# Third down pass of a SwiGLU block: unit 8 as seven half-size products in three of four column groups, gated sums added to the residual in DRAM

## The chip, the cores and the metric

The kernel runs on one core of a Trainium2 chip. The metric is device time in microseconds of one execution of the whole program. All matrix work is in float32, each operand cut into a high and a low part, so that one product of the reference is three matmuls on the chip (high by high, high by low, low by high).

## The reference

One layer of a bidirectional encoder: adaLN modulation, two attention mixers with gates, an output projection, and a SwiGLU channel mixer, over 512 tokens of width 2048. What matters here is its end:

```python
h2 = rms_norm(x, norm2_w[l]) * (1.0 + sc2) + sh2
ff = (jax.nn.silu(h2 @ w_ffn_gate[l]) * (h2 @ w_ffn_up[l])) @ w_ffn_down[l]
x = x + g2 * ff
return rms_norm(x, final_w)
```

`w_ffn_down` has 5632 rows and 2048 columns. `g2` is one row of 2048 numbers, the same for all tokens.

## The kernel before

**Units and column groups.** The 5632 hidden features are eleven units of 512 (0 to 10). The gated hidden values of a unit are written to DRAM (`ff_d`) by the gate and up stage. The down projection goes over them in four passes: units 0 and 1, units 2 to 5, units 6 to 9, and unit 10. Each of the first three passes goes over four column groups `cc` of 512 output columns each. A pass keeps its sum of one group (`acc`, 512 tokens by 512 columns, 1 MB) in the accumulators of PSUM, adds it to what the passes before left, and passes 1 and 2 store it to `acc_d[cc]` in DRAM. The third pass loads it again (line 1585), adds its own products, multiplies by `g2` and adds the residual `x2_d`.

**Plain units and seven-product units.** `down_group` (line 1414) does one pass over one group. A unit named in `ss` is done in the Strassen-Winograd way: the 512 by 512 hidden block and the 512 by 512 weight block are cut into quarters, and seven products of sums of quarters replace eight products of quarters. Each product is 12 matmuls of 256 columns (two of each direction, times three for the high and low parts), so such a unit is 84 matmuls, and a plain one (`plain`, line 1433) is 96. For a plain unit the weights are loaded in two transfers of 512 KB and split into high and low (`wsplit`, lines 168 and 170: ACT copies the high part, DVE subtracts for the low part). For a seven-product unit `wforms` (line 686 on) loads the same two transfers, makes four sums of quarters on DVE (lines 696 to 699) and splits four pieces, one of 512 elements a partition and three of 1024. The hidden side of such a unit is made once for all groups by `sforms` (line 1384): two loads of 512 KB, four sums (lines 1393 to 1396), four splits, into a slot that holds the result. It is a generator with two steps; the list `bg` holds those under way, and `pump` advances it by one step after every piece of work.

**Slots and areas.** There are three slots for seven-product forms. In the second pass they hold units 2, 3 and 4; units 6 and 7 take over slots 0 and 1 in its last group, and in the third pass slot 2 is free: its room is used by `xr` (a residual group and two `g2` factors) and by `fl` (the split hidden values of unit 10). Two areas hold the split hidden values of plain units (5, 8, 9).

**Order within the third pass.** Group 0 does the plain units 8 and 9 first (`lead`) and then 6 and 7; groups 1 to 3 do 6, 7 and then the plain units 8 and 9 (`tail`). While the tail runs on TensorE, DVE adds the seven products of the finished units to `acc` (lines 1471 to 1480), and after the tail four more sums (line 1485). `late(cc)` gives a function that `down_group` calls after each unit; it starts what belongs to the stage behind. In particular, after unit 7 of the next group `gated_sum` runs for the group before: two multiplications of `acc` by the factor (line 1576) and two additions of the residual (line 1577), each 128 partitions by 1024 elements; then the sum is stored to `x2p_d[cc]` (line 1579) and the next residual group and factor are loaded (lines 1569, 1570). In group 3 the stage behind is prepared: the `g2` row for all columns (`rows`, line 439), the three stored sums are loaded again (line 1557), and the weights of unit 10 are multiplied by `g2` (line 1528) and split. The last stage (line 1612 on) then does unit 10 for all columns, adds to `x2`, normalises and writes out.

**What sets the order.** Weights are loaded on SP's queue, the hidden values, `acc`, the residual and the factors on POOL's queue, each in the order of its instructions, and an instruction that waits holds up those behind it. A planner orders each engine's instructions by priority and its own costs; `high_priority` moves work ahead, and `behind` (an alias of `keep_in_program_order`) and `issue_after` tie it down. Five buffers hold loaded weights (`raw`, also used for loaded hidden values) and five hold split ones (`whl`); a seven-product unit needs two and four of them, a plain one two and two.

Of the kernel before, what the change touches and what calls it, by code (L numbers as in the profile page):

```python
# [20 lines left out]
P = 128  # L21
# [91 lines left out]
def encoder_block(ctx: ExitStack, tc, xp, xT, c, ada1_w, ada2_w, b_ada, norm1_w, w_in, q_norm_w, k_norm_w, bias,  # L113
# [1404 lines left out]
    xr = p_e.tile([P, 3072 + 64], F32, tag="s23072", name="xr")  # L1518
    xo = [xr[:, :2048].rearrange("p (i n) -> p i n", i=NT)]
    fl = p_e.tile([P, 4096 + 64], F32R, tag="s24096", name="fl")  # L1520
    wl = {}
    x2p_d = [dram.tile([P, NT, 512], F32, name=f"x2pd{cc}") for cc in range(3)]
# [9 lines left out]
    def late(cc):  # L1532
        def behind(u):
            if cc == 0 and u == 8:
                while bg:
                    pump()
            if cc == 1 and u > 7:
                a = u - 8
                xl_pairs.append(ff_pair(10, a, [fl[:, a * 2048 + e * 1024:a * 2048 + (e + 1) * 1024] for e in range(2)],
                                        pin=tc.keep_in_program_order))  # L1540
# [6 lines left out]
            if cc == 3 and u == 7:  # L1547
                x2.append(p_s.tile([P, NT, 512], F32, tag="s13072", name="xd"))
                gf = p_s.tile([P, 2, D], F32, tag="s14096", name="gf")
                wide2.extend((gf[:, 0], gf[:, 1]))  # L1550
                rows(wide2[0], g2_d)
            if cc == 3 and u == 9:
# [3 lines left out]
                for c in range(3):  # L1556
                    nc.gpsimd.dma_start(x2[c], x2p_d[c])
# [7 lines left out]
    def factor(cc):  # L1565
        return xr[:, 2048 + cc % 2 * 512:2560 + cc % 2 * 512]

    def residual_of(cc):
        nc.gpsimd.dma_start(xo[0], x2_d[:, cc * 512:(cc + 1) * 512].rearrange("(i p) d -> p i d", p=P))
        nc.gpsimd.dma_start(factor(cc), g2_d[cc].partition_broadcast(P).rearrange("p o d -> p (o d)"))  # L1570

    def gated_sum(cc, acc):
        to = xo[0] if cc < 3 else x2[3]
        for t in range(2):
            ts = slice(2 * t, 2 * t + 2)
            behind(V.tensor_mul(acc[:, ts], acc[:, ts], factor(cc).unsqueeze(1).to_broadcast([P, 2, 512])))
            behind(V.tensor_add(to[:, ts], xo[0][:, ts], acc[:, ts]))
        if cc < 3:
            nc.gpsimd.dma_start(x2p_d[cc], xo[0])
            residual_of(cc + 1)  # L1580

    residual_of(0)
    for cc in range(4):
        acc = acc_tile()
        nc.gpsimd.dma_start(acc, acc_d[cc])
        down_group(cc, (6, 7), cl, acc, late(cc), () if cc else (8, 9), late=cc > 1,
# [6 lines left out]
    for cc in range(2, 4):  # L1593
        wt = p_s.tile([P, 4096 + 64], F32R, tag=f"a{3 - cc}", name=f"w{cc}")
# [80 lines left out]
```

## Time and profile before

| what | value |
|---|---|
| median of three runs | 2465.59 us (2464.08 to 2469.82) |
| the profiled execution | 2474.1 us, span of its instructions 2472.3 us |
| TensorE busy (PE) | 2435.4 us, 99% of the span |
| DVE busy | 2007.5 us, 81% |
| ACT busy | 1069.9 us, 43% |
| granted TensorE clock, mean | 0.997 of full |
| DMA, mean over the span | 187 GB/s |

The profiled execution is 8.5 us longer than the median of the runs. The span runs from the first to the last instruction of the program; the remaining 1.8 us lie around it. The chain of waits is followed back from the last instruction; its shares tell which engine held the end, averaged over the whole program, not what holds it in the third pass. That is read from stretches of the trace. The passes were placed in it by the names of the operands of the matmuls (`s` for seven-product units, `a` for plain ones, `fl` for unit 10): the second pass begins with the first products at 2100.7 us, the third at 2258.1 us, and the last stage at 2418.9 us.

### The profile page before, as it was taken

What the parts mean: (1) busy time and instruction counts of PE and PEld (TensorE: products, weight loads), DVE (VectorE), ACT (ScalarE), POOL (GpSimd) and SP (SyncE); (2) the same over time, 40 slices, a digit from 0 to 9 for tenths busy, and PEclk for the clock granted to TensorE, in tenths of its full rate; (3) what the DMA queues carried; (4) which work ended last, traced back from release to release, by engine and by line L of the source; (5) the groups of instructions that cost most, each with busy time, mean ns of one, the idle gap of its engine ahead of it and who ended that gap; (6) DMA issues with size and microseconds to landing.
All of it is one profiled execution on the core that took longest, in us unless ns stands there. A gap on an engine that the chain in (4) does not pass through costs nothing.

```text
span 2472.3 us, 42367 instructions
## 1 busy us (share of the span) xinstructions
PE 2435.4 (99%) x17327; PEld 2280.1 (92%) x17327; DVE 2007.5 (81%) x2704; ACT 1069.9 (43%) x1466; POOL 150.9 (6%) x255
## 2 busy tenths in 40 slices
PE   7999999999999999999999999999999999999998
PEld 6888888999888888888999999999999998999997
DVE  7995778999677678667899989889989885687877
ACT  5223455544344523237744444444444454433333
POOL 0100000000011111111000000000000010000010
PEclk9999999999999999999999999999999999999999
DMA  9874322455766687867444444445454466546563
GB/s 357 285 253 144 104 89 80 142 185 181 252 211 231 204 302 248 296 215 228 137 154 155 145 162 147 135 147 163 129 171 147 128 196 214 188 155 233 189 250 121
DMA packets 213730, 461.77 MB, mean 187 GB/s; under 512 B 15152, under 2 KB 59552, under 8 KB 204832
## 3 DMA queue, kind: packets, MB, share of 16 engines
q1 hardware_dynamic: 174160, 309.76, 38.4%
q0 software_dynamic: 29872, 132.73, 15.8%
q10 hardware_dynamic: 9504, 16.58, 1.9%
q8 instruction: 136, 2.23, 0.4%
q14 instruction: 58, 0.48, 0.1%
HBM read 412.84 MB, written 46.17 MB: 186 GB/s over the span
## 4 chain that ended last, share of the span: by engine, by line
PE 72%; DVE 14%; issue 6%; DMA 4%; ACT 1%; POOL 0%; DVEq 0%; POOLq 0%; ACTq 0%
PE mm L190 15%; PE mm L189 15%; PE mm L188 15%; PE S L188 6%; PE S L189 6%; PE S L190 6%; DVE whl L170 4%; PE Y L188 3%; PE Y L189 2%; PE Y L190 2%; DVE raw L524 2%; DMA raw<-in_w_down 2%; DMA raw<-in_w_up 1%; PE T L886 1%; DVE g_acc L631 1%
## 5 line engine op out<-in xcount | busy, mean ns | idle before, releaser
L168 ACT ACTIVATE whl<-raw 128x1024 fp32r<-128x1024 f32 (+1 forms) x483 | 453.9, 943 | 671.1 <-PE mm L190 288.4
L170 DVE TENSOR_TENSOR whl<-raw,whl 128x1024 fp32r<-128x1024 f32 (+1 forms) x483 | 517.9, 1087 | 126.3 <-ACT whl L168 125.9
L168 ACT ACTIVATE whl<-ta 128x1024 fp32r<-128x1024 f32 x124 | 131.4, 1059 | 181.8 <-PE mm L190 107.6
L168 ACT ACTIVATE whl<-tb 128x1024 fp32r<-128x1024 f32 x124 | 131.4, 1060 | 174.5 <-PE S L190 109.8
L170 DVE TENSOR_TENSOR whl<-ta,whl 128x1024 fp32r<-128x1024 f32 x124 | 151.2, 1220 | 40.7 <-ACT whl L168 40.1
L388 DVE SCALAR_TENSOR_TENSOR acc<-mw,cact,acc 128x1024 f32<-128x1024 f32 x124 | 158.8, 1281 | 18.3 <-DMA mw<-in_ada_w 17.9
L170 DVE TENSOR_TENSOR whl<-tb,whl 128x1024 fp32r<-128x1024 f32 x124 | 150.9, 1217 | 4.6 <-ACT whl L168 4.5
L366 POOL DMA_DIRECT2D mw<-in_ada_w x113 | 60.3, 534 | 1361.5 <-DVE acc L388 946.5
L697 DVE TENSOR_TENSOR ta<-raw,ta 128x512 f32<-128x512 f32 x124 | 85.2, 687 | 69.3 <-DMA raw<-in_w_down 29.7
L696 DVE TENSOR_TENSOR ta<-raw 128x512 f32<-128x512 f32 x124 | 85.3, 688 | 36.7 <-DMA raw<-in_w_down 34.3
L188 PE MATMUL mm<-x56h,whl 128*128 128x256 f32 x336 | 92.5, 275 | 0.4 <-DVE c L784 0.4
L189 PE MATMUL mm<-x56l,whl 128*128 128x256 f32 x336 | 92.4, 275 | 0.0
L190 PE MATMUL mm<-x56h,whl 128*128 128x256 f32 x336 | 92.4, 275 | 0.0
L189 PE MATMUL mm<-whl,s 128*128 128x256 f32 x320 | 88.2, 276 | 1.0 <-DVE whl L170 0.8
L188 PE MATMUL mm<-x3h,whl 128*128 128x256 f32 x320 | 88.1, 275 | 0.0
L188 PE MATMUL mm<-whl,s 128*128 128x256 f32 x320 | 88.1, 275 | 0.0
L189 PE MATMUL mm<-x3l,whl 128*128 128x256 f32 x320 | 88.0, 275 | 0.0
L190 PE MATMUL mm<-x3h,whl 128*128 128x256 f32 x320 | 88.0, 275 | 0.0
L188 PE MATMUL S<-x56h,whl 128*128 128x256 f32 x320 | 88.0, 275 | 0.0
L189 PE MATMUL S<-x56l,whl 128*128 128x256 f32 x320 | 88.0, 275 | 0.0
L190 PE MATMUL S<-x56h,whl 128*128 128x256 f32 x320 | 88.0, 275 | 0.0
L190 PE MATMUL mm<-whl,s 128*128 128x256 f32 x320 | 88.0, 275 | 0.0
(1879 smaller groups left out, 8910.9 us busy)
## 6 DMA issues: line engine op xcount, KB each, us to landing
raw<-in_w_in SPq DMA_DIRECT2D x133, 512.0 KB, 4.6
mw<-in_ada_w POOLq DMA_DIRECT2D x113, 512.0 KB, 4.5
raw<-in_w_gate SPq DMA_DIRECT2D x92, 512.0 KB, 4.6
raw<-in_w_up SPq DMA_DIRECT2D x88, 512.0 KB, 4.6
raw<-in_w_down SPq DMA_DIRECT2D x88, 512.0 KB, 5.4
raw<-in_ada_w POOLq DMA_DIRECT2D x29, 1024.0 KB, 6.6
raw<-in_w_out SPq DMA_DIRECT2D x48, 512.0 KB, 5.5
ffd<-c SPq DMA_DIRECT2D x10, 1024.0 KB, 4.8
```

The lines of the kernel that those rows point to most:

```text
L168: high = pin(S.activation(hi, src, AF.Copy))
L170: latest[:] = [high, pin(eng.tensor_sub(lo, src, hi))]
L188: nc.tensor.matmul(o, lh, rh, start=start, stop=False, **kw)
L189: nc.tensor.matmul(o, lh, rl, start=False, stop=False, **kw)
L190: nc.tensor.matmul(o, ll, rh, start=False, stop=stop, **kw)
L366: mod["queue"].dma_start(w, ada2_w[n * P:(n + 1) * P, :])
L388: behind(V.scalar_tensor_tensor(acc, part, cact[:, k:k + 1], acc, op0=ALU.mult, op1=ALU.add))
L524: V.scalar_tensor_tensor(raw, raw, 1.0, call, op0=ALU.mult, op1=ALU.mult, accum_out=y)
L631: V.tensor_add(acc, acc, b)
L696: V.tensor_sub(t1, b12, b11)
L697: V.tensor_sub(t2_, b22, t1)
L886: nc.tensor.transpose(tp[:, k * P:(k + 1) * P], e[:, k * P:(k + 1) * P], ident)
```

## The change

- In groups 1 to 3 of the third pass unit 8 is done as seven products after units 6 and 7; only unit 9 stays plain there. Group 0 keeps units 8 and 9 plain, in front. The forms of unit 8 are made by `sforms` into slot 2; it is put into `bg` after unit 7 of group 0.
- `gated_sum` no longer adds on DVE for groups 0 to 2: after each multiplication a DMA on POOL's queue stores that half of `acc` (512 KB) with an addition into `x2_d`. The loads of the residual groups into `xr` and the stores to `x2p_d` go away. For group 3 DVE adds to a residual group that is loaded into `x2[3]` after unit 7 of group 3.
- The three other groups of `x2` are loaded from `x2_d` (rows of 2 KB) instead of `x2p_d` (8 KB a partition).
- `fl` moves to the area that held unit 8, and one of the last stage's weight tiles to slot 2; the factors get two small buffers of their own.

```diff
-    xr = p_e.tile([P, 3072 + 64], F32, tag="s23072", name="xr")
-    xo = [xr[:, :2048].rearrange("p (i n) -> p i n", i=NT)]
-    fl = p_e.tile([P, 4096 + 64], F32R, tag="s24096", name="fl")
-    wl = {}
-    x2p_d = [dram.tile([P, NT, 512], F32, name=f"x2pd{cc}") for cc in range(3)]
+    fl, wl = [], {}
+    x2_of = lambda cc: x2_d[:, cc * 512:(cc + 1) * 512].rearrange("(i p) d -> p i d", p=P)
...
+            if cc == 0 and u == 7:
+                bg.append(sforms(2, 8))
             if cc == 1 and u > 7:
                 a = u - 8
-                xl_pairs.append(ff_pair(10, a, [fl[:, ...
+                if a == 0:
+                    fl.append(p_s.tile([P, 4096 + 64], F32R, tag="a1", name="fl"))
+                xl_pairs.append(ff_pair(10, a, [fl[0][:, ...
...
                 rows(wide2[0], g2_d)
+                nc.gpsimd.dma_start(x2[3], x2_of(3))
...
-                    nc.gpsimd.dma_start(x2[c], x2p_d[c])
+                    nc.gpsimd.dma_start(x2[c], x2_of(c))
...
-    def factor(cc):
-        return xr[:, 2048 + cc % 2 * 512:2560 + cc % 2 * 512]
-
-    def residual_of(cc):
-        nc.gpsimd.dma_start(xo[0], x2_d[:, cc * 512:(cc + 1) * 512].rearrange("(i p) d -> p i d", p=P))
-        nc.gpsimd.dma_start(factor(cc), g2_d[cc].partition_broadcast(P).rearrange("p o d -> p (o d)"))
+    def factor_of(cc):
+        f = p_e.tile([P, 512], F32, tag="g2f", name="g2f", bufs=2)
+        nc.gpsimd.dma_start(f, g2_d[cc].partition_broadcast(P).rearrange("p o d -> p (o d)"))
+        factors.append(f)
 
     def gated_sum(cc, acc):
-        to = xo[0] if cc < 3 else x2[3]
+        f = factors.pop(0).unsqueeze(1).to_broadcast([P, 2, 512])
         for t in range(2):
             ts = slice(2 * t, 2 * t + 2)
-            behind(V.tensor_mul(acc[:, ts], acc[:, ts], factor(cc).unsqueeze(1).to_broadcast([P, 2, 512])))
-            behind(V.tensor_add(to[:, ts], xo[0][:, ts], acc[:, ts]))
+            behind(V.tensor_mul(acc[:, ts], acc[:, ts], f))
+            if cc == 3:
+                behind(V.tensor_add(x2[3][:, ts], x2[3][:, ts], acc[:, ts]))
+            else:
+                nc.gpsimd.dma_start(x2_of(cc)[:, ts], acc[:, ts], accum_op=ALU.add)
         if cc < 3:
-            nc.gpsimd.dma_start(x2p_d[cc], xo[0])
-            residual_of(cc + 1)
+            factor_of(cc + 1)
...
-        down_group(cc, (6, 7), cl, acc, late(cc), () if cc else (8, 9), late=cc > 1,
+        down_group(cc, (6, 7, 8) if cc else (6, 7), {9: cl[9]} if cc else cl, acc, late(cc), () if cc else (8, 9), late=cc > 1,
                    after_lead=cc == 1)
...
-        wt = p_s.tile([P, 4096 + 64], F32R, tag=f"a{3 - cc}", name=f"w{cc}")
+        wt = (p_e if cc == 2 else p_s).tile([P, 4096 + 64], F32R, tag="s24096" if cc == 2 else "a0", name=f"w{cc}")
```

More of the change, by code (lines that the diff above doesn't have):

```diff
@@ L1536, in behind @@
                     pump()
+            if cc == 0 and u == 7:
+                bg.append(sforms(2, 8))
             if cc == 1 and u > 7:
                 a = u - 8
-                xl_pairs.append(ff_pair(10, a, [fl[:, a * 2048 + e * 1024:a * 2048 + (e + 1) * 1024] for e in range(2)],
+                if a == 0:
+                    fl.append(p_s.tile([P, 4096 + 64], F32R, tag="a1", name="fl"))
+                xl_pairs.append(ff_pair(10, a, [fl[0][:, a * 2048 + e * 1024:a * 2048 + (e + 1) * 1024] for e in range(2)],
                                         pin=tc.keep_in_program_order))
@@ L1563, in encoder_block @@
     due = []
-    def factor(cc):
-        return xr[:, 2048 + cc % 2 * 512:2560 + cc % 2 * 512]
-    def residual_of(cc):
-        nc.gpsimd.dma_start(xo[0], x2_d[:, cc * 512:(cc + 1) * 512].rearrange("(i p) d -> p i d", p=P))
-        nc.gpsimd.dma_start(factor(cc), g2_d[cc].partition_broadcast(P).rearrange("p o d -> p (o d)"))
+    def factor_of(cc):
+        f = p_e.tile([P, 512], F32, tag="g2f", name="g2f", bufs=2)
+        nc.gpsimd.dma_start(f, g2_d[cc].partition_broadcast(P).rearrange("p o d -> p (o d)"))
+        factors.append(f)
     def gated_sum(cc, acc):
-        to = xo[0] if cc < 3 else x2[3]
+        f = factors.pop(0).unsqueeze(1).to_broadcast([P, 2, 512])
         for t in range(2):
             ts = slice(2 * t, 2 * t + 2)
-            behind(V.tensor_mul(acc[:, ts], acc[:, ts], factor(cc).unsqueeze(1).to_broadcast([P, 2, 512])))
-            behind(V.tensor_add(to[:, ts], xo[0][:, ts], acc[:, ts]))
+            behind(V.tensor_mul(acc[:, ts], acc[:, ts], f))
[3 more added lines that the diff above has]
+                nc.gpsimd.dma_start(x2_of(cc)[:, ts], acc[:, ts], accum_op=ALU.add)
         if cc < 3:
-            nc.gpsimd.dma_start(x2p_d[cc], xo[0])
-            residual_of(cc + 1)
-    residual_of(0)
+            factor_of(cc + 1)
+    factors = []
+    factor_of(0)
     for cc in range(4):
```

## The prediction

> **What bounds the kernel now.** I read the page first, then busy time by stretches, then who waited for whom in the passes concerned, then the groups of DVE instructions, then the DMA issues.
>
> ```profile
> span 2472.3 us, 42367 instructions
> PE 2435.4 (99%) x17327; PEld 2280.1 (92%) x17327; DVE 2007.5 (81%) x2704; ACT 1069.9 (43%) x1466; POOL 150.9 (6%) x255
> PE 72%; DVE 14%; issue 6%; DMA 4%; ACT 1%; POOL 0%; DVEq 0%; POOLq 0%; ACTq 0%
> ```
>
> TensorE bounds the whole program, but that is an average. The third pass is the next view: its four column groups and the last stage (span, then PE, weight loads, DVE, ACT, POOL busy, granted clock, DMA share, GB/s).
>
> ```profile
> 2258.10:2298.30 40.20, 40.20 (x362) 40.20 (x361) 30.82 (x40) 15.82 (x17) 1.61 (x3) 1.00 0.60 202
> 2298.30:2338.50 40.20, 40.20 (x362) 40.20 (x361) 35.39 (x44) 14.34 (x15) 2.91 (x5) 1.00 0.59 204
> 2338.50:2378.70 40.20, 40.20 (x362) 40.20 (x361) 30.96 (x39) 12.44 (x13) 2.39 (x4) 1.00 0.56 200
> 2378.70:2418.90 40.20, 40.20 (x362) 40.20 (x361) 28.84 (x30) 13.65 (x14) 5.03 (x9) 1.00 0.80 294
> 2418.90:2472.30 53.40, 42.23 (x206) 36.51 (x204) 42.33 (x81) 17.32 (x44) 0.00 (x0) 0.95 0.25 87
> ```
>
> In all four groups PE is busy for the whole stretch at full clock: the third pass is bound by matmuls, with nothing else in the way. So matmuls taken out there are worth their own time, as long as nothing else becomes late. DVE is at 72% to 88% of a group.
>
> The second pass already has the shape that the change gives to groups 1 to 3: three seven-product units and one plain unit. Its groups 1 to 3, and a piece of the last one:
>
> ```profile
> 2135.65:2176.07 40.42, 39.39 (x350) 39.00 (x349) 29.52 (x40) 14.14 (x15) 1.06 (x2) 1.00 0.48 160
> 2176.07:2215.33 39.26, 39.12 (x350) 38.93 (x349) 29.62 (x39) 14.08 (x15) 2.13 (x4) 1.00 0.48 161
> 2215.33:2258.10 42.77, 41.02 (x350) 40.64 (x349) 36.58 (x46) 19.09 (x21) 5.02 (x9) 0.96 0.69 229
> 2234.60:2238.00 3.40, 3.40 (x18) 0.51 0.96 327
> ```
>
> Who PE waited for in the second pass (total, times, longest):
>
> ```profile
> PE S L189 <- DVE whl L170: 1.1, 2, 0.9
> PE S L188 <- ACT whl L168: 0.9, 1, 0.9
> PE mm L189 <- DVE whl L170: 0.8, 1, 0.8
> PE T L662 <- ACT acc L1490: 0.7, 1, 0.7
> ```
>
> So in this shape PE does wait, for split weights (`whl`) of a seven-product unit.
>
> **The change, part by part.**
>
> *Matmuls.* A group of the third pass is 2 x 84 + 2 x 96 = 360 matmuls in 40.20 us, 0.1117 us each. With unit 8 as seven products it is 3 x 84 + 96 = 348, or 38.86 us. That is 1.34 us a group and 4.0 us for three: the whole of what can be gained on PE.
>
> *DVE work.* The rows of the third pass:
>
> ```profile
> L170 DVE TENSOR_TENSOR whl<-raw,whl 128x1024 fp32r<-128x1024 f32 x25 | 30.1, 1217 | 6.2 <-ACT whl L168 6.2
> L170 DVE TENSOR_TENSOR whl<-ta,whl 128x1024 fp32r<-128x1024 f32 x8 | 9.7, 1218 | 2.8 <-ACT whl L168 2.8
> L1577 DVE TENSOR_TENSOR xr<-xr,acc 128x1024 f32<-128x1024 f32 x6 | 7.3, 1222 | 0.1
> L696 DVE TENSOR_TENSOR ta<-raw 128x512 f32<-128x512 f32 x8 | 5.5, 688 | 8.4 <-DMA raw<-in_w_down 8.3
> L170 DVE TENSOR_TENSOR whl<-raw,whl 128x512 fp32r<-128x512 f32 x8 | 5.5, 683 | 0.0
> ```
>
> A seven-product unit costs DVE four sums of 0.69, one split of 0.68 and three of 1.22 us: 7.1 us. A plain unit costs two splits, 2.4 us. So each of groups 1 to 3 gains 4.7 us of DVE work. Each loses the two additions of line 1577, 2.4 us. The forms of unit 8 cost 7.1 us once (the same four sums and four splits), between unit 7 of group 0 and unit 7 of group 1. By the stretches above: groups 0 and 1 together go from 66.2 to 66.2 + 7.1 + 4.7 - 2.4 = 75.6 us of DVE in 40.20 + 38.86 = 79.06 us, 96%; group 2 to 33.3 us in 38.86 (86%); group 3 to 31.1 us (80%). On average DVE still fits. What decides is whether it fits before each unit starts, with five `whl` buffers against four that a unit needs.
>
> *What that costs in group 1.* Upper bound: group 3 of the second pass, which made the forms of two units beside three seven-product units and took 42.77 us for 348 matmuls, 3.9 us above 38.86. Of this 1.7 us is the half clock in the 3.4 us from 2234.6 (18 matmuls where 30 fit), and 2.2 us is waiting. Lower bound: 0, as 75.6 us do fit in 79. I take the middle, 2.0 us.
>
> The Trainium skill ("TensorE: Matmul & The Clock Gate", section "What's actually happening") says that the array falls to half rate after an idle window of about 3.4 us. Here it fell after waits of 2.2 us in all, so the measurement decides; the 3.4 us at half rate do agree with that window. By the page's rule the bound above would be 2.2 us, and the middle 1.1.
>
> *What it costs in groups 2 and 3.* The same shape without forms lost 40.42 - 38.86 = 1.6 us in group 1 of the second pass and 0.4 us in group 2. I take these two for the two groups, 2.0 us together; bounds 0 (DVE ahead in time) and 3.9 each (as above). The two multiplications of line 1576 come on top there, but their time is free to choose, since nothing but the store waits for them.
>
> *ACT.* Copies of high parts rise by about the same number of elements as the splits do; at 12 to 16 us of 40 it has room. Zero; were it late, DVE's splits would be late with it, which the bounds above hold.
>
> *The DMAs.* Taken out per group 0 to 2: a 1 MB load of the residual and a 1 MB store. Put in: two stores of 512 KB that add. The issues of the third pass (KB each, median us to landing), and GB/s in 40 slices of 4 us:
>
> ```profile
> GB/s 191 258 355 186 320 194 6 251 13 253 6 68 197 49 310 307 395 405 274 29 133 257 6 19 280 361 376 410 60 98 104 193 41 393 382 392 364 412 384 275
> raw<-in_w_down SPq DMA_DIRECT2D x35, 512.0 KB, 5.4
> acc<-accd POOLq DMA_DIRECT2D x3, 1024.0 KB, 7.9
> x2pd<-xr POOLq DMA_DIRECT2D x3, 1024.0 KB, 5.2
> xr<-x2d POOLq DMA_DIRECT2D x3, 1024.0 KB, 10.5
> xa<-x2pd POOLq DMA_DIRECT2D x2, 1024.0 KB, 7.4
> ```
>
> No trace shows an adding store. Bounds for 1 MB: 5.2 us (a plain store) and 5.2 + 10.5 = 15.7 us (store plus a read of those rows); I take the upper end, since the old contents have to be read. Behind it on POOL's queue stand the next factor, the load of `acc` two groups on (it now waits for the landing, as it fills the same buffer) and hidden values of unit 10. `acc` is first needed some 40 us later, so 15.7 us are covered; without that cover group cc + 2 would stand at its first sum.
>
> The Trainium skill ("Collectives: The Full Stack", section on the bandwidth ceiling) says that an add in the DMA path reads two sources and so halved a measured rate (62.28 against 32.35 GB/s). It speaks against the change; by it the store costs as 2 MB do, some 10 us, inside my bounds.
>
> *The start of the last stage.* The last seven slices above are at 275 to 412 GB/s: here DMA is full for 28 us. The waits of DVE from 2401.9 to 2424.1 and of PE from 2418.9 show it:
>
> ```profile
> DVE raw L1528 <- DMA raw<-in_w_down: 3.8, 4, 2.4
> DVE raw L1528 <- DMA gf<-g2d: 3.3, 1, 3.3
> ...
> PE S L189 <- DVE whl L170: 1.0, 1, 1.0
> PE mm L189 <- DVE w L170: 0.3, 1, 0.3
> ```
>
> PE waits 1.3 us for weights that DVE got late from DMA. The stretch opens when unit 6 of group 3 is done, which comes 2 x 1.34 = 2.7 us earlier, while PE arrives 4.0 us earlier: 1.3 us more to wait. That is the value I take. Below: the wait goes, -1.3 us. Above: 1.3 plus the read of the old 1 MB at 390 GB/s, 2.7 us, 4.0 us in all. The seven sums of group 3 also move behind unit 8, into the idle time of DVE shown here.
>
> *Sum.* -4.0 + 2.0 + 2.0 + 1.3 = +1.3 us. The durations are of one execution of 2474.1 us, 8.5 above the median; the difference is laid on the median: 2465.6 + 1.3 = 2466.9 us. The 0.2% that a measurement tells from no change is 4.9 us: 2460.7 to 2470.5. The forecast is no change, as PE gives up in waits what it saves in matmuls.
>
> **The rivals.**
>
> *The saving stays (2461.6 us, or 2460.3 with the last wait gone).* For it: in the gate and up stage DVE is as full, and PE does not wait:
>
> ```profile
> 1800.00:1900.00 100.00, 99.78 (x893) 99.60 (x892) 89.83 (x111) 43.41 (x47) 2.65 (x5) 1.00 0.49 157
> ```
>
> Against it: that stage has DMA at half and no hidden forms or sums of groups in between; the second pass, which has them, waits at 75% of DVE.
>
> *DVE becomes the bound in all three groups (slower, 2474.6 us).* Place: the splits of unit 8. Between the first form of unit 6 and the last of unit 8 DVE has 21.3 us of forms, 12 sums of a group at 0.69 (8.3 us) and the multiplications (2.4 us): 32 us against 28.1 us of PE. It decides if the lead that DVE takes from the plain unit is under 4 us, as the buffers may make it. Price: 3.9 us in each group, with the half clock: -4.0 + 11.7 + 1.3 = +9.0. Against it: two groups of the second pass lost only 0.4 and 1.6.
>
> *The adding store is slow and the last stage waits for the residual (2472 us).* The sums of group 2 are stored in group 3, and `x2` is read behind that. In the trace the first use of the third residual group is here:
>
> ```profile
> 2435.14 0.69 DVE L1608 TENSOR_TENSOR xb<-xb,ro 128x512 f32<-128x512 f32 x1
> ```
>
> The second multiplication of group 2 ends at about 2391.5. With 15.7 us for the store and 10.5 us for the load it is there by 2418, 17 us early. A store of 30 us or more with several such loads in a row would come some 5 us too late: -4.0 + 4.0 + 1.3 + 5 = +6 or so. No row speaks for that price.
>
> **How the numbers follow.** Forecast (within some 3.5 us of 2466.9): 0.47. The saving stays: 0.27. DVE bound: 0.15. Slow store: 0.11. Faster by over 0.2% needs the first rival with the last wait gone as well: 0.10. Slower by over 0.2%: nearly all of the third and fourth case: 0.22. Within: 0.68. The range goes from below the first rival's time, 2461.0, to 2473.0, short of the DVE-bound case, which leaves out about 2 in 10.
>
> **What would show it.** Right: groups 1 to 3 with 348 matmuls each; PE waits on line 170 of 1 to 3 us in group 1, under 2 in each other; a wait at the start of the last stage of 2 to 3 us. A granted clock near 0.5 for 3.4 us in group 1 would mean the upper bound there. Wrong: no PE wait on line 170 in the third pass (the first rival), waits of 2 us and half clock in all three groups (the second), DVE waiting on line 1608 for a DMA of `x2` (the third), or adding stores that land later than 16 us.

## The result and the profile after

The changed kernel takes 2496.12 us (median of 4 runs, 2493.19 to 2500.70) against 2466.61 us for the kernel before on the same chip: a ratio of 1.0121, with a 95% interval of 1.0100 to 1.0141. It is slower by some 30 us, and the forecast of no change is wrong.

The page of the kernel after: the span, the busy time of each engine, and the chain of waits by engine.

```profile
span 2495.6 us, 42337 instructions
PE 2437.1 (98%) x17291; PEld 2280.6 (91%) x17291; DVE 2018.6 (81%) x2724; ACT 1077.7 (43%) x1476; POOL 156.7 (6%) x257
PE 77%; DVE 13%; issue 3%; DMA 3%; ACT 1%; POOL 0%; DVEq 0%; POOLq 0%; ACTq 0%
```

The profile holds 36 matmuls fewer, three times 12, as the change says, and yet PE is not less busy: part of its work ran at a lower clock. The page alone does not say where the 23 us of span went. Busy time by stretches does: group 0, groups 1 to 3 and the last stage (span, then PE, weight loads, DVE, ACT, POOL, granted clock, DMA share, GB/s).

```profile
2253.60:2293.80 40.20, 40.20 (x363) 40.20 (x361) 30.81 (x40) 15.98 (x18) 2.12 (x4) 1.00 0.59 196
2293.80:2337.19 43.39, 40.62 (x350) 40.42 (x349) 36.03 (x48) 16.75 (x18) 4.74 (x6) 0.96 0.63 177
2337.19:2380.70 43.51, 41.02 (x350) 40.64 (x349) 32.99 (x43) 14.07 (x15) 3.61 (x4) 0.96 0.59 163
2380.70:2438.96 58.26, 41.92 (x350) 41.54 (x349) 34.87 (x41) 16.05 (x17) 7.75 (x10) 0.85 0.67 208
2438.96:2495.60 56.64, 43.92 (x206) 37.77 (x204) 43.56 (x82) 16.23 (x43) 0.00 (x0) 0.91 0.24 84
```

Before, the five took 40.20 four times and 53.39. So group 1 costs 3.2 us more, group 2 3.3, group 3 18.1 and the last stage 3.3: 27.8 us from the start of the third pass to the end. (The third pass starts 4.5 us earlier here than in the profile of before, which was an execution 8.5 us above its median. Of this, 4.0 us lie in the second pass, which the change leaves alone: it takes 158.6 us here and 162.6 us there, where its first product starts at 2095.5 us, not at 2100.7 as I wrote above. So I compare from the start of the third pass on.)

Group 3 is the question. Who PE waited for in groups 1 to 3, then who DVE waited for (total, times, longest):

```profile
PE Y L189 <- DVE whl L170: 15.2, 1, 15.2
PE Y L188 <- DVE acc L1485: 3.4, 2, 2.3
PE mm L189 <- DVE whl L170: 3.0, 2, 2.8
```

```profile
DVE raw L1525 <- DMA gf<-g2d: 21.9, 1, 21.9
DVE fl L170 <- ACT fl L168: 7.0, 1, 7.0
```

One wait of PE is 15.2 us long, and behind it is one wait of DVE of 21.9 us: line 1525, the product of unit 10's weights with the row of `g2` (`gf`). DVE's instructions in order of time show what stands behind it in its queue (start, duration, what, and in brackets the idle time ahead and what ended it):

```profile
2399.54 1.22 DVE L170 TENSOR_TENSOR whl<-tb,whl 128x1024 fp32r<-128x1024 f32 x1
2422.70 1.23 DVE L1525 TENSOR_TENSOR raw<-raw,gf 128x1024 f32<-128x1024 f32 x1 [21.94 <-DMA gf<-g2d]
2423.85 0.68 DVE L1471 TENSOR_TENSOR acc<-acc,p 128x512 f32<-128x512 f32 x1
2424.45 2.35 DVE L170 TENSOR_TENSOR whl<-raw,whl 128x1024 fp32r<-128x1024 f32 x2
```

The product is wanted only in the last stage, but the splits of unit 9 (2424.45), for which PE stands still in group 3, come behind it. And this is why the row is late, POOL's queue in the same time:

```profile
2392.10 0.77 POOL L1559 DMA_DIRECT2D xa<-x2d  x1 [20.47 <-PE mm L190]
2399.51 1.21 POOL L1580 DMA_DIRECT2D x2d<-acc  x1 [6.63 <-DVE whl L170]
2409.59 1.23 POOL L1580 DMA_DIRECT2D x2d<-acc  x1 [8.86 <-issue]
2416.11 0.80 POOL L1559 DMA_DIRECT2D xa<-x2d  x1 [5.30 <-issue]
2416.90 1.69 POOL L439 DMA_DIRECT2D gf<-g2d  x3
2421.92 0.54 POOL L439 DMA_DIRECT2D gf<-g2d  x1 [3.33 <-issue]
```

A load of the residual, two adding stores, another load, and only then the row. The stores and the second load each go out 0.3 us after the landing of the transfer ahead (landings at 2399.19, 2409.25 and 2415.80 us). The profile does not say so: it puts 8.86 and 5.30 us to "issue", which means to nothing that it shows, and 6.63 us to a split on DVE. In the kernel before, the first part of the row went out 3.1 us behind the store ahead of it, before that store had landed (2402.07 us):

```profile
2393.64 0.54 POOL L1579 DMA_DIRECT2D x2pd<-xr  x1 [3.93 <-DVE xr L1577]
2396.69 1.60 POOL L439 DMA_DIRECT2D gf<-g2d  x3 [2.52 <-PE S L190]
```

In groups 1 to 3 of the kernel after, the adding stores of 512 KB take this long from issue to landing (times issued, KB, median us):

```profile
x2d<-acc POOLq DMA_DIRECT2D x6, 512.0 KB, 6.3
```

### The profile page after: what moved, and what is told of

It is laid out like the page before. It is cut to its first block, busy times and chain, and to the rows that moved or that the text cites. A ratio compares the mean times of both kernels' runs of the same rounds, so it can differ in the third digit from the quotient of the medians.

```text
span 2495.6 us, 42337 instructions
## 1 busy us (share of the span) xinstructions
PE 2437.1 (98%) x17291; PEld 2280.6 (91%) x17291; DVE 2018.6 (81%) x2724; ACT 1077.7 (43%) x1476; POOL 156.7 (6%) x257
## 4 chain that ended last, share of the span: by engine, by line
PE 77%; DVE 13%; issue 3%; DMA 3%; ACT 1%; POOL 0%; DVEq 0%; POOLq 0%; ACTq 0%
PE mm L190 16%; PE mm L189 16%; PE mm L188 16%; PE S L188 6%; PE S L190 6%; PE S L189 6%; DVE whl L170 4%; PE Y L188 3%; PE Y L189 3%; PE Y L190 3%; DVE raw L524 2%; DMA raw<-in_w_down 1%; PE T L886 1%; DMA raw<-in_w_up 1%; PE T L190 1%
## 5 line engine op out<-in xcount | busy, mean ns | idle before, releaser
L388 DVE SCALAR_TENSOR_TENSOR acc<-mw,cact,acc 128x1024 f32<-128x1024 f32 x124 | 158.8, 1281 | 19.9 <-DMA mw<-in_ada_w 19.5
L189 PE MATMUL mm<-whl,s 128*128 128x256 f32 x368 | 102.7, 279 | 3.0 <-DVE whl L170 3.0
L188 PE MATMUL mm<-whl,s 128*128 128x256 f32 x368 | 102.2, 278 | 0.0
L190 PE MATMUL mm<-whl,s 128*128 128x256 f32 x368 | 102.1, 277 | 0.0
```

Source lines behind the costliest of these rows:

```text
L188: nc.tensor.matmul(o, lh, rh, start=start, stop=False, **kw)
L189: nc.tensor.matmul(o, lh, rl, start=False, stop=False, **kw)
L190: nc.tensor.matmul(o, ll, rh, start=False, stop=stop, **kw)
L388: behind(V.scalar_tensor_tensor(acc, part, cact[:, k:k + 1], acc, op0=ALU.mult, op1=ALU.add))
```

## The experiments

All edits are to the kernel after unless said otherwise. The theories, by the letters of the expectations: A, the adding stores go to the same tensor `x2_d` as the loads behind them, so each waits for the last; B, DVE has too much work; B1, the forms of unit 8 fill DVE at the start of group 1; C, adding stores fill the DMA engines; D, POOL's queue has room for only so many descriptors, and rows of 2 KB need many; E, an adding store always waits for the one before; F, only the order of DVE's instructions matters. G to J came later and are told in their expectations.

The table gives for each run the lengths of the stages, cut at the first matmul of each by its operand, their sum from the start of the third pass to the end, and the ratio of the medians to the kernel before with its interval (`e4` was run once).

```
                          grp 0 grp 1 grp 2 grp 3 last    sum    ratio
before                    40.20 40.20 40.20 40.20 53.39 | 214.19
after                     40.20 43.39 43.51 58.26 56.66 | 242.02 1.0121 [1.0100, 1.0141]
e1_factor_on_act          40.20 43.88 43.54 39.44 67.79 | 234.85 1.0101 [1.0084, 1.0118]
e2_residual_tiles         40.20 42.94 44.30 54.40 60.38 | 242.22 1.0129 [1.0114, 1.0145]
e3_plain_store            40.20 43.23 41.53 38.86 65.32 | 229.14 1.0083 [1.0063, 1.0103]
e4_no_forms               40.20 38.86 41.32 55.82 59.11 | 235.31
e5_adding_store_only      40.20 40.20 40.20 44.78 68.26 | 233.64 1.0099 [1.0084, 1.0114]
e6_sevens_only            40.20 44.28 39.77 42.67 63.63 | 230.55 1.0081 [1.0064, 1.0097]
e8_ring_2048              40.20 43.63 47.21 47.52 59.44 | 238.00 1.0121 [1.0106, 1.0136]
e9_rows_4k                40.20 45.49 41.37 45.71 59.05 | 231.82 1.0085 [1.0070, 1.0100]
e10_rows_act_early        40.20 38.86 45.63 40.18 60.57 | 225.44 1.0073 [1.0058, 1.0088]
e11_row_product_later     40.20 42.82 43.63 44.33 63.97 | 234.96 1.0111 [1.0094, 1.0128]
e12_adding_store_4k_act   40.20 40.20 40.20 40.20 58.17 | 218.97 1.0031 [1.0021, 1.0041]
e13_forms_early           40.20 38.86 44.92 58.17 57.15 | 239.30 1.0116 [1.0101, 1.0131]
e14_rows_no_store         40.20 40.20 40.20 40.20 51.57 | 212.37 1.0010 [1.0000, 1.0019]
e15_early_no_store        40.20 39.70 43.88 38.86 58.31 | 220.95 1.0038 [1.0023, 1.0053]
e16_rows_xb_behind        40.20 40.20 40.20 40.20 58.48 | 219.28 1.0038 [1.0026, 1.0050]
e17_early_xb_behind       40.20 40.29 45.30 40.13 60.19 | 226.11 1.0066 [1.0048, 1.0085]
e18_no_sums               40.20 39.30 42.90 39.11 56.65 | 218.16 1.0024 [1.0011, 1.0037]
```

348 matmuls at full clock are 38.86 us, 360 are 40.20. Each row is one execution, and code that no edit touches varies too: the second group of the second pass takes 38.86 us in the trace of `e12` and 43.38 us in that of `e18`. So one or two us in one group tell nothing by themselves.

### Is it the queue? The row of `g2` on ACT's queue

```diff
-    def rows(dst, src):
+    def rows(dst, src, queue=None):
...
-                rows(wide2[0], g2_d)
+                rows(wide2[0], g2_d, nc.scalar)
```

> The changed kernel with one edit: the four loads of the g2 row for all columns (line 439, ahead of the last stage) are issued on ACT's queue instead of POOL's. Theory A (the row stands in POOL's queue behind transfers on x2_d that wait for each other's landing, and the first multiplication by it holds DVE's queue): the 15.2 us wait of PE in group 3 goes, group 3 falls from 58.3 us to 41 to 45, the whole to about 2481 (2477 to 2486). Theory B (DVE has too much work with three seven-product units): the wait stays, 2496. Theory C (the adding stores fill the DMA engines so that every load is late): the row lands late on any queue, wait over 8 us, 2490 or more.

Group 3 falls from 58.26 to 39.44 us: the 15.2 us wait is gone. But the last stage takes 67.79 us, and only 7 of 19 us stay gained; the whole, 2487.8 us, lies just above the range of theory A. Who DVE waited for there, and who PE waited for:

```profile
DVE xd L1578 <- DMA xd<-x2d: 9.3, 1, 9.3
```

```profile
PE mm L188 <- ACT w L168: 12.5, 1, 12.5
```

Now the residual of group 3 (`xd`), still on POOL's queue, is late; DVE stands at its addition, and the last weights' products and splits stand behind that. The queue is late as a whole, not the one row.

### What makes the queue late? Tensors, plain stores, room

```diff
-    x2_d = dram.tile([T, D], F32, name="x2d")
+    x2_d = [[dram.tile([T // 2, 512], F32, name=f"x2d{cc}{t}") for t in range(2)] for cc in range(4)]
```

(and the stores and loads of `x2_d` go by its eight parts)

> The changed kernel with the residual x2_d kept in DRAM as eight tensors (column group by token half) instead of one, so that an adding store waits for no other transfer of the residual; two loads of 512 KB replace each of 1 MB. Theory A: POOL's queue no longer stands, the g2 row and the hidden values of unit 10 are loaded earlier; group 3 falls from 58.3 us to 41 to 45 and group 2 from 43.5 to 40 to 42.5, the whole to about 2479 (2475 to 2485). Theory B: both stay, 2496. Theory C: as many bytes are added, so 2490 or more.

```profile
2352.14 1.22 POOL L1584 DMA_DIRECT2D x2d<-acc  x1 [31.39 <-DVE acc L1580]
2358.51 1.23 POOL L1584 DMA_DIRECT2D x2d<-acc  x1 [5.15 <-issue]
```

Nothing is gained. The second store of group 1, to a tensor of its own, still goes out 6.4 us behind the first, with 5.15 us of idle time for "issue". Theory A falls.

```diff
-                nc.gpsimd.dma_start(x2_of(cc)[:, ts], acc[:, ts], accum_op=ALU.add)
+                nc.gpsimd.dma_start(aside_d[cc][t], acc[:, ts])
```

> The changed kernel, but the six stores of gated sums are plain stores of the same size into DRAM tensors of their own; the addition to the residual of groups 0 to 2 is left out, so the output lacks it. Theory A: like the kernel with eight residual tensors, about 2479 (2475 to 2485), and a store of 512 KB lands in 3 to 5 us where the adding one took 6.2 to 9.7. Theory B: 2496. Theory C: much faster than with eight residual tensors, by 8 us or more, since the adding itself is gone.

The sum falls by 12.9 us to 229.14, and the time is 11.4 us below that of `e2`, as theory C expected. The stores as plain ones to tensors aside take this long (512 KB, same columns as above):

```profile
asd<-acc POOLq DMA_DIRECT2D x6, 512.0 KB, 3.9
```

An adding store takes 1.6 times as long (6.3 us). With little else under way it is 6.2 us (issued 2310.86, landed 2317.07) against 2.9 us (2311.03, 2313.91). But this is not the adding alone: the tensors aside have rows of 4 KB, `x2_d` has rows of 2 KB. With rows of 4 KB (`e9`, below) the first adding store of group 0 takes 5.4 us (2307.46, 2312.89), 1.9 times the plain one. The Trainium skill ("Collectives: The Full Stack", section on the bandwidth ceiling) has a factor of 1.93 between the measured rates of a copying and an adding collective; the 1.9 of this case agrees. Group 3 is free of waits, and still the last stage takes 65.32 us: without any adding store the trace has the loads with rows of 2 KB go out one at a time (issued 2388.42, 2396.71 and 2408.43, the second and third 0.3 us after the landing of the one before). So it is not only the adding stores, and this run does not tell the adding from the shorter rows.

```diff
-        f = p_e.tile([P, 512], F32, tag="g2f", name="g2f", bufs=2)
+        f = p_e.tile([P, 512], F32, tag="g2f", name="g2f", bufs=1)
...
-    nc = bacc.Bacc(... dynamic_dma_scratch_size=1024)
+    nc = bacc.Bacc(... dynamic_dma_scratch_size=2048)
```

> The changed kernel with the memory that POOL's queue has for the descriptors of its DMAs doubled from 1024 to 2048 bytes a partition; to make room the small factor tile has one buffer instead of two. With eight residual tensors the second adding store still waited for the landing of the first, and loads of rows of 2 KB waited for each other though nothing of theirs conflicts. Theory D (POOL's queue stands because the descriptors of transfers in rows of 2 KB fill that memory, the adding ones above all): transfers follow each other sooner, the g2 row is issued 8 us or more earlier, PE's wait in group 3 falls from 15.2 to under 6 us, the whole to 2478 to 2488. Theory E (an adding store always waits for the landing of the one before, whatever the room): the second store of each pair still issues only after the first has landed, 2490 to 2498.

```profile
2399.64 2.45 POOL L1580 DMA_DIRECT2D x2d<-acc  x2
2405.65 0.79 POOL L1559 DMA_DIRECT2D xa<-x2d  x1 [2.97 <-issue]
2406.75 1.11 POOL L439 DMA_DIRECT2D gf<-g2d  x2 [0.30 <-PE S L190]
```

With twice the room for descriptors both stores go out one behind the other, 1.1 us apart, and the row's issue comes 18 us after the start of group 3, against 36 us in the kernel after. So the silent wait of the second store was for room: D is right on the mechanism, and E falls. But the time does not move (1.0121): the trace has the row land 14 us after its issue (2406.75 to 2420.76), behind the transfers ahead of it on the same queue. In place of the one long wait PE has several of up to 6.0 us, and D's range for the whole is missed.

```diff
-    x2_d = dram.tile([T, D], F32, name="x2d")
+    x2_d = [[dram.tile([P, 2, 512], F32, name=f"x2d{cc}{t}") for t in range(2)] for cc in range(4)]
```

> The changed kernel with the residual in DRAM as eight tensors of 128 rows of 4 KB each (column group by token half, laid out as in SBUF), instead of rows of 2 KB, so that loads and adding stores of 512 KB have half the pieces; the stores that first write the residual, long before, are cut in two. Theory D: half the descriptors, so the same relief as with doubled room: the g2 row 8 us or more earlier, PE's wait in group 3 under 6 us, 2478 to 2488. Theory E: the stores of a pair still follow one another by landing; loads may gain a little; 2488 to 2497.

Rows of 4 KB in place of 2 KB, which is half as many pieces. (The Trainium skill, "DMA: Bandwidth & Descriptors", section "Why a DMA increments its semaphore by 16 and not by 1", says that one descriptor moves one contiguous run; the smaller need for room agrees with it.) The stores go out 1.14 us apart, and the row is issued at 2394.40 us, 18 us after the start of group 3 as in `e8`:

```profile
2388.04 0.91 POOL L1585 DMA_DIRECT2D x2d<-acc  x1 [1.16 <-DVE acc L1581]
2389.18 0.89 POOL L1585 DMA_DIRECT2D x2d<-acc  x1 [0.23 <-issue]
2394.40 1.08 POOL L439 DMA_DIRECT2D gf<-g2d  x2 [2.49 <-PE S L190]
```

This is worth 10.2 us of the 27.8, within D's range, where more room alone gained 4.0 us in the sum and nothing in the ratio; eight tensors alone gained nothing (`e2`). What makes the difference is not settled: of the 6.2 us between `e8` and `e9`, 5.8 lie in group 2, and `e8` also has one buffer for the factors where there were two.

### Is it DVE's order or its load?

```diff
-            V.tensor_mul(r3, r3, wide2[0][:, ...
+            behind(V.tensor_mul(r3, r3, wide2[0][:, ...
```

> The changed kernel with the multiplications of unit 10's weights by the g2 row (line 1525) pinned into program order, so that on DVE the first one stands behind the splits of unit 9 and the first sum, no longer ahead of them; the queues of POOL and SP are the same. Theory F (it is the place on DVE's queue ahead of unit 9's splits that makes PE wait, and the late row alone would be covered): group 3 falls from 58.3 us to 41 to 45, the last stage stays at 56 to 58, the whole about 2482. Theory D (the row itself comes too late): group 3 falls as much, but the last stage waits in its place, 62 to 70 us, the whole 2486 to 2495.

Group 3 falls by 13.9 us and the last stage grows by 7.3: part of the wait moves to where its result is used. The order on DVE is where the wait shows, not its cause; F explains 7 of 28 us.

```diff
-                bg.append(sforms(2, 8))
+                sx[8] = sx[4]
```

> The changed kernel without the forms of unit 8: no loads, sums and splits of sforms(2, 8); the products of unit 8 in groups 1 to 3 read the old forms in that slot, so the output lacks the right unit 8 there. Theory B1 (the forms and the third unit's sums fill DVE at the start of group 1): the wait of 3 us at the start of group 1 goes and group 1 falls from 43.4 us to 39 to 40.5. Rival (the wait is from the third unit alone): group 1 stays over 42. Group 3 keeps its wait of over 10 us by both.

```diff
             if cc == 0 and u == 8:
                 while bg:
                     pump()
+                bg.append(sforms(2, 8))
-            if cc == 0 and u == 7:
-                bg.append(sforms(2, 8))
```

> The changed kernel with the forms of unit 8 put into the background list one unit later than unit 8 of group 0 has been done, that is between the two plain units at the head of the third pass, where DVE stands idle for some 12 us, instead of after unit 7 of group 0. Theory B1 (the forms fill DVE just when the first splits of group 1 are due): group 1 falls from 43.4 us to 39 to 41, the wait of 3 us at its start goes, the rest stays: 2490 to 2494. Rival (the third unit's splits are too much wherever the forms stand): group 1 stays over 42.

Group 1 is 38.86 us in both, without a wait; here groups 1 and 2 of the kernel with the forms of unit 8 begun three units earlier:

```profile
2288.88:2327.74 38.86, 38.86 (x351) 38.86 (x349) 31.58 (x41) 15.30 (x17) 4.20 (x5) 1.00 0.65 183
2327.74:2372.66 44.92, 41.81 (x351) 40.86 (x350) 33.56 (x44) 14.59 (x16) 3.61 (x4) 0.96 0.56 158
```

So the whole of the 4.5 us above 38.86 in group 1 came from the place of the forms (B1). Group 2 is 1.4 us longer, too little to be read by itself; from `e9` to `e10` below, where the forms move too, it is 4.3 us longer. Group 3 stays as in the kernel after, at 58.17: early forms alone gain 2.7 us in the sum, and the ratios (1.0116 against 1.0121) do not tell this from nothing.

### Each half of the change by itself

The kernel before, with the adding stores but unit 8 plain everywhere:

```diff
-            behind(V.tensor_add(to[:, ts], xo[0][:, ts], acc[:, ts]))
+            if cc == 3:
+                behind(V.tensor_add(x2[3][:, ts], x2[3][:, ts], acc[:, ts]))
+            else:
+                nc.gpsimd.dma_start(x2_of(cc)[:, ts], acc[:, ts], accum_op=ALU.add)
...
```

> The kernel before with only the second half of the change: gated sums of groups 0 to 2 are added in DRAM by the storing DMA, the residual of group 3 is loaded into x2[3]; unit 8 stays plain in all groups. Theory A: the g2 row is late by the same chain of transfers, PE waits in group 3 for 8 to 15 us with no seven-product unit 8 there; 2474 to 2484. Theory B: no such wait, 2463 to 2468. Theory C: as A, with DMA engines over 90% busy in the wait.

```profile
DVE raw L1526 <- DMA gf<-g2d: 20.9, 1, 20.9
```

The stores by themselves cost 19.5 us (233.64 against 214.19), and make DVE wait 20.9 us for the same row, without one seven-product unit more. That is theory A's chain, but the time is lost in another place than it said: 4.6 us in group 3 and 14.9 in the last stage.

The change with the addition left on DVE (residual group and factors in the area that held unit 8, `fl` loaded in group 3):

```diff
-                nc.gpsimd.dma_start(x2_of(cc)[:, ts], acc[:, ts], accum_op=ALU.add)
+                behind(V.tensor_add(to[:, ts], xo[0][:, ts], acc[:, ts]))
...
-            if cc == 1 and u > 7:
+            if cc == 3 and u > 7:
```

> The first half of the change alone: unit 8 as seven products in groups 1 to 3, with the gated sums added by DVE and stored to x2p_d in 8 KB pieces, as before. For room the residual group sits in the area that unit 8 leaves, and the hidden values of unit 10 are loaded in group 3 into the slot that unit 8's forms leave, not in group 1. Theory D: no wait of over 5 us in group 3; the sevens cost what the prediction said, waits of 2 to 5 us a group against 1.3 us saved; 2463 to 2474. Theory B (DVE): waits of 8 us and more in group 3 even without the adding stores, 2478 or more.

Group 2 takes 39.77 us where it took 43.51, with neither an adding store nor `fl`'s load in front of it. In the kernel after, DVE stood 7.0 us for `fl` (the second row of DVE's waits above), whose load is behind two adding stores on POOL's queue. The last stage (63.63 us) is not to be compared, since `fl` is loaded late there. Theory D holds in that group 3 has no wait over 5 us, but the whole, 2484.1 us, lies above its range; with the last stage mixed up in this way the run gives no price for the seven products.

### Mending what was found

Rows of 4 KB, the row of `g2` on ACT's queue, forms early; all three edits are shown above.

> The whole change with the three cures together: residual in rows of 4 KB, g2 row on ACT's queue, forms of unit 8 early. By theories B1 and D group 1 takes 39 to 41 us, groups 2 and 3 40 to 43, the last stage 54 to 58: 2464 to 2475, at best level with the kernel before. If a further cause stands behind them, 2478 or more.

The sum falls by 16.6 us to 225.44; 11.3 us above before remain, in group 2 (45.63) and in the last stage (60.57). The time, 2482.9 us, says by the expectation that a further cause stands behind the three.

The kernel of `e5` with rows of 4 KB and the row of `g2` on ACT's queue:

> The adding store alone (unit 8 plain in all groups), with the residual in rows of 4 KB and the g2 row on ACT's queue. Theory D (the price of the adding store is the room and the order on POOL's queue): no wait over 3 us in group 3 or at the start of the last stage, 2461 to 2469, against 2486.5 for the adding store alone as the change has it. Theory C (adding in DRAM itself takes the DMA engines): waits of over 6 us stay at the start of the last stage, 2474 or more.

No wait is left in groups 1 to 3, but the last stage keeps 4.8 us more than before, with a wait of 3.6 us in it; 2471.9 us lies between the ranges of D and C. Two explanations were left for it, the adding stores' traffic (G) and the loads of the residual, which now go out in one bunch (H).

```diff
-                nc.gpsimd.dma_start(x2_of(cc, t), acc[:, ts], accum_op=ALU.add)
+                pass
```

> The adding store alone, with rows of 4 KB and the row of g2 on ACT's queue, but the adding stores of groups 0 to 2 are left out (their gated sums are computed and go nowhere, so the residual lacks three quarters of the down product of units 0 to 9). With the stores the last stage took 58.17 us against 53.39 before. Theory G (what the adding stores move crowds the last weights out): the last stage falls to 53 to 54.5 us and the sum from the third pass's start to 214 to 216 us. Theory H (the loads of the residual, which now come in one go, crowd them out): the last stage stays at 57 us or above, the sum at 217.5 or above.

> The adding store alone, with rows of 4 KB and the row of g2 on ACT's queue; the load of the third residual group (1 MB) moved from POOL's queue behind the last weights on SP's. Theory H: the last weights land earlier, the last stage falls from 58.17 to 54 to 56 us and the sum to 215 to 217. Theory G: 1 MB less ahead of the weights helps as much as 1 MB less of stores would, so it too expects a fall, but only if the 1 MB was ahead of them: below 1.5 us.

(`e16`: the loads of `x2[2]` go from POOL's queue to SP's, behind the last weights.) Without the stores the last stage takes 51.57 us, 6.6 less, and with the load moved 58.48: G, not H, though the fall is larger than G said. The DMA view of `e12` and then of `e14` from group 3 on, loads of weights and of the residual:

```profile
raw<-in_w_down SPq DMA_DIRECT2D x9, 512.0 KB, 6.3
xa<-x2d POOLq DMA_DIRECT2D x4, 512.0 KB, 11.8
xb<-x2d POOLq DMA_DIRECT2D x2, 512.0 KB, 16.1
xd<-x2d POOLq DMA_DIRECT2D x2, 512.0 KB, 16.5
```

```profile
raw<-in_w_down SPq DMA_DIRECT2D x9, 512.0 KB, 5.9
xa<-x2d POOLq DMA_DIRECT2D x4, 512.0 KB, 7.0
xb<-x2d POOLq DMA_DIRECT2D x2, 512.0 KB, 7.2
xd<-x2d POOLq DMA_DIRECT2D x2, 512.0 KB, 9.3
```

Only 1 MB of adding stores lies in this window, and every 512 KB of residual takes 5 to 9 us longer to land (medians). The medians of the weights hide what counts: the last of them lands 5.4 us after the first matmul of the last stage in `e12` (2415.92 against 2410.54 us), and 0.2 us after it in `e14` (2414.55 against 2414.39). Since `e14` leaves out the whole store, it does not tell the adding from the storing: plain stores in its place were not tried.

The same two edits to `e10`:

> Seven products in three groups, forms early, rows of 4 KB, the row of g2 on ACT's queue; the adding stores are left out (the residual lacks the same part). With the stores group 2 took 45.63 us, the last stage 60.57, the sum 225.44. Theory G: group 2 falls to 39 to 41 us, the last stage to 55 to 57, the sum to 215 to 219. Theory I (the seven products themselves overload DVE and the weight buffers): group 2 stays at 44 us or above. Theory H: the last stage stays at 59 or above.

> The same move in the kernel with seven products, early forms, rows of 4 KB and the row of g2 on ACT's queue. Groups 1 to 3 as they were (38.9, 45.6, 40.2, within 1.5 us each). Theory H: the last stage falls from 60.57 to 56 to 58 us. Theory G: by under 1.5 us.

Leaving the stores out gains 4.5 us (225.44 to 220.95), moving the load nothing (226.11). What is left is the price of the seven products alone, `e15` against `e14`: 8.6 us, where PE saves 4.0. Group 2 still takes 43.88 us, just under what I expected and far above G's 39 to 41, and the last stage 58.31. But in group 2 DVE is not overloaded: it stands for loaded weights, 4.7 us in one go (a load issued at 2349.91 and landed at 2356.81), and PE 1.8 us behind it. In groups 1 to 3 of `e15`:

```profile
DVE ta L696 <- DMA raw<-in_w_down: 8.0, 2, 4.9
DVE ta L697 <- DMA raw<-in_w_down: 6.5, 2, 4.7
```

Nor do three seven-product units alone make group 2 slow: `e6` has them too, with late forms and `fl` loaded in group 3, and takes 39.77 us. All five versions with early forms take 42.90 to 45.63 us there. Whether the place of the forms or that of `fl`'s load makes the difference was not tried. The last stage is another matter. DVE in the 29.4 us from the first product with the row of `g2`, in `e15` and then in `e14` (same columns as the stretches above):

```profile
2397.20:2426.60 29.40, 25.41 (x183) 23.56 (x182) 29.38 (x33) 8.48 (x8) 0.00 (x0) 0.95 0.47 176
```

```profile
2399.00:2428.40 29.40, 29.40 (x205) 27.68 (x204) 25.25 (x26) 9.85 (x12) 0.00 (x0) 1.00 0.44 166
```

With seven products DVE has not 0.1 us to spare, and without them 4.2 us. If that is the cause, work taken from DVE there should help:

```diff
+            if cc < 3 or 8 not in ss:
...
-            V.tensor_add(a[0][0], a[0][0], p1)
+                V.tensor_add(a[0][0], a[0][0], p1)
...
```

(so indented are all eight sums)

> As e15_early_no_store (no adding stores), and of group 3 the eight sums of 0.68 us that DVE makes of the seven products' banks between units 8 and 9 are left out (5.5 us of DVE work; column group 3 of the output lacks units 6 to 8). In e15 DVE was busy for 29.38 of the 29.40 us from 2397.20, and the last stage took 58.31 us against 51.57 with unit 8 in eight products. Theory I (DVE is full from the landing of the row of g2 to the last weights, and what moved there makes the last weights late): the last stage falls by 4 to 6.5 us, to 52 to 54.5. Theory J (the last weights are late because their buffer, which held unit 8's forms, comes free late): the last stage stays at 57 or above. Group 2, which is not touched, stays at 43 to 45.

The last stage takes 56.65 us, 1.7 less, which misses I's range and lies just under J's 57; so small a difference between two executions may also be chance. DVE's waits from group 3 on tell why it is no more:

```profile
DVE raw L1531 <- DMA gf<-g2d: 6.2, 1, 6.2
DVE raw L1531 <- DMA raw<-in_w_down: 4.3, 2, 4.1
```

DVE now waits for weights instead. In the trace of `e14` four loads of weights went out 27.5 to 21.3 us ahead of the last stage; in `e15` two did, 25.5 and 24.3 us ahead, and the next two 11.3 and 10.1. The buffers for loaded weights come free later beside seven products. That the buffers hold the rest is read from these times; a run with more of them was not made.

## Why the prediction was wrong

*Matmuls, -4.0 us.* Right. Groups 1 and 3 reached 38.86 us in some run where nothing held them (`e4`, `e13`, `e10` in group 1, `e3` and `e15` in group 3); group 2 came to 39.77 us at best (`e6`).

*Group 1, +2.0 us.* The mechanism was right, the size was off: 4.5 us above 38.86. I bounded it at 3.9 by a group of the second pass and took the middle because 75.6 us of DVE work fit into 79 on average. They don't fit in time: the forms and the first weights of group 1 come together, and the same work three units earlier cost group 1 nothing. The average was no guide at all: DVE was busy for 66.8 us in groups 0 and 1 (30.81 + 36.03), less than I counted, and late all the same. I also misread the group behind the bound: its rows show 1.75 us without a matmul (42.77 - 41.02), not 2.2 us of waiting. The clock near 0.5 that I named as the sign of the upper bound is in the trace, behind the wait of 2.8 us, first row of busy time by stretches here:

```profile
2298.20:2301.20 3.00, 3.00 (x14) 3.00 (x15) 3.00 (x6) 0.00 (x0) 0.53 (x1) 0.50 0.40 128
2322.90:2330.00 7.10, 7.10 (x66) 7.10 (x65) 0.11 (x2) 1.12 (x2) 0.54 (x1) 1.00 1.00 323
```

*Groups 2 and 3, +2.0 us together.* Group 2 alone lost 4.7 us. The second row shows how it began, at the end of group 1: DVE idle for 7 us with the DMA engines at 1.00, the wait for `fl`; the sums that free a bank for PE came behind it, and PE waited 2.3 us for them at 2345.47 (the second row of PE's waits above). I counted DVE's instructions and not what each waits for. With no store at all (`e15`) group 2 still lost 5.0, by another wait, for loaded weights, so my 2.0 was too low here as well; what part the place of the forms has in it stays open. The 1.6 and 0.4 us that I took were of one execution, too: the same two groups of the second pass lost nothing in `e12`, 4.5 and 0.6 in `e18`.

*The DMAs: this step failed.* Its price held: I took 15.7 us for 1 MB of adding stores, and two of 512 KB take 12.6 one after the other. What failed is the sentence on who stands behind them. I named the next factor, `acc` and unit 10's hidden values, found `acc` covered for 40 us, and stopped. The row of `g2` and three residual loads stand behind them on the same queue in group 3, and unit 9's splits stand behind that row on DVE's. The queue also holds less than I took for granted: before, a residual load had rows of 2 KB too, but the stores and final loads went in 8 KB a partition, so few pieces were under way at once. Now every transfer of the residual is in rows of 2 KB, and one store of 512 KB leaves no room for the next. This step was worth 0 in the sum. By the runs it is 19.5 us on its own (`e5`); of that, 14.7 go with rows of 4 KB and the row on another queue (`e12`), and the rest, with 1.8 more, when the stores go (`e14`).

*The start of the last stage, +1.3, bound +4.0.* It measured +3.3 after, inside the bound, but by chance: much of the lateness was already spent in group 3. In `e12`, where nothing is late before, it is 4.8 us, more than my bound of 2.7 us for the extra read plus 1.3. And the sums of group 3 did not move into idle time of DVE: about half of that idle time (3.3 of 7.1 us) was a wait for the same row, and once it lands DVE is full (`e15`).

*The rivals.* That the saving stays was wrong by 35 us. The slow adding store was the right transfer with the wrong victim: the last stage did not wait for the residual first, group 3 did, for the row behind it, and at a price per store of 6.3 us, not 30. DVE as the bound in all three groups is not what the profile after shows. When the DMA trouble is gone the seven products cost 8.6 us, and that this is near the 9.0 of this rival is luck: they lie in group 2 and in the last stage and not in each group, and for part of them DVE waits for weights.

What the whole is made of, from the sums of the table: rows of 4 KB 10.2 us, the row on another queue with early forms 6.4, the adding stores 4.5, the seven products 8.6. That is 29.7 us down to 212.37 (`e14`), 1.8 below before. By the medians, each against before on its own chip, the four are 8.4, 3.4, 8.2 and 7.5 us, so they are known to some 3 us. `e14` has no stores at all, so it is no version to use. The parts are not independent: `e5` and `e6`, each half alone, cost 19.5 and 16.4, together more than the 27.8 of both.

Still open: the medians of all versions, with rows of 2 KB too, lie higher above before than their sums do, by 1.7 to 6.4 us. `e14` is 1.8 us below before in the sum and 2 us above it in the median. The one trace of before is of an execution 8.5 us above its median, so its last stage may usually be shorter than 53.39 us, or the versions may lose time ahead of the third pass; that was not tried. No version beat the kernel before.

## What to carry to other kernels

Before a transfer is added to a queue, list all that stands behind it until the program's end, and for each who waits for it and what stands behind that on its engine; a landing time says nothing of this. A transfer on POOL's queue costs room by its number of rows as well as time by its bytes, so keep a tensor that is stored and read back in long rows. Work that fits an engine on average must be checked at the places where two bursts meet: the same forms cost group 1 4.5 us or nothing, by where they stood, though group 2 gave part of it back.

## What the runs showed of the hardware

- A transfer on POOL's queue that finds no room for its descriptors waits in silence: the profile puts the idle time to "issue" (8.86 us) or to an engine that was done long ago (6.63 us to a split on DVE). With the setting at 1024 a second 512 KB store in rows of 2 KB waited for the landing of the first (2399.51 and 2409.59 us; landing at 2409.25), with 2048 or with rows of 4 KB it followed after 1.1 us.
- An adding store of 512 KB with rows of 4 KB took 5.4 us and a plain one with the same rows 2.9 us, each with the next store 1.1 us behind it (`e9`, `e3`); with rows of 2 KB an adding one took 6.2 us.
- Queues that are in order pass a wait on: a row that DVE stood 21.9 us for, needed only in the stage behind, cost PE 15.2 us.
